# A two-layer recurrent decoder step on one Trainium2 core: the RWKV scans placed link by link between dense products

## The chip, the cores and the metric

The kernel runs on one core of one Trainium2 chip. The core has five engines, each with an instruction stream of its own that it works through in order: TensorE (PE in the profile: matmuls, and PEld for the weight loads beside them), VectorE (DVE), ScalarE (ACT), GpSimd (POOL) and SyncE (SP), which here issues DMAs. They wait for one another by semaphores. The metric is the device time of one execution in microseconds, the median of three runs.

## The reference, cut to what matters

One step of a decoder trunk of two layers for 1024 prompt tokens of a new sequence and 8 sampled tokens, in float32, model width 1024. Layer 0 mixes by Mamba-2 and mLSTM, layer 1 by RWKV-7; each is followed by a SwiGLU of width 2816. The change touches the RWKV-7 scan of the prompt tokens (16 heads of 64):

```python
def _rwkv7_mixer(xn, shift, wkv, p, j):
    x_prev = jnp.concatenate([shift[:, None].astype(xn.dtype), xn[:, :-1]], axis=1)
    xr, xw, xk, xv, xa, xg = (xn + (x_prev - xn) * mu[c] for c in range(6))
    r, k, v = xr @ p['rw_wr'][j], xk @ p['rw_wk'][j], xv @ p['rw_wv'][j]
    ...                                  # decay w, rate a, gate g: low-rank products of xw, xa, xg
    kk = k * p['rw_k_k'][j]; kk = kk / jnp.maximum(jnp.sqrt(jnp.sum(kk * kk, -1, keepdims=True)), 1e-12)
    k = k * (1 + (a - 1) * p['rw_k_a'][j])
    # per head and token, S is 64 x 64 (value x key):
    #   sa = S @ -kk;  S = S * w + sa (kk * a)^T + v k^T;  y = S @ r
    y, new_s = _rwkv7_scan(r, decay, k, v, kk, a, wkv)
    y = (y - mean) * lax.rsqrt(var + RWKV_LN_EPS) * p['rw_ln_w'][j] + p['rw_ln_b'][j]
    y = (y + bonus) * g                  # bonus = sum(r * k * r_k) * v, per head
    return y @ p['rw_wo'][j], (xn[:, -1], new_s)

def _swiglu(x, w_gu, w_down):
    gate, up = jnp.split(x @ w_gu, 2, axis=-1)
    return (jax.nn.silu(gate) * up) @ w_down
```

## The kernel before, in words

**Tokens and stages.** The tokens are worked in two halves, 0 (tokens 0 to 511) and 1 (512 to 1031, the sampled ones among them). In program order: layer 0's mixer for both halves, `ffn(0,0)` (layer 0, half 0), the RWKV projections of half 0 (`rwkv_proj(0)`), `ffn(0,1)`, `rwkv_proj(1)`, `rwkv_out(0)` (output projection of half 0), `ffn(1,0)`, in whose course `rwkv_out(1)` is written at its 21st row block, then `ffn(1,1)` and the final norms.

**Dense products.** Every weight tile of 128 x 128 and every activation is split into a high and a low fp32r part, and a product is three matmuls (`mm3`, L186: low·high, high·low, high·high). `dense_tile` (L189) writes, for one output tile of 128 rows and each block of columns (2 x 260 or 2 x 256 for a half), one chain of eight such terms, 24 matmuls, into a PSUM bank, and then the operations that empty it. The splitting of weights is done by ACT (high, L175) and DVE (low, L145). In an `ffn`, names are `ps_g`, `ps_u` (gate, up), `ps_d` (down, fed by `al`, `ah`, the split of silu(gate)·up), `xb`/`xc` (the residual that `ps_d` is added to), and `f01l`, `f10l` and so on (the normed input).

**The scan of a half** has 16 heads as 8 pairs j (two heads fill 128 partitions), and 8 chunks of 64 tokens. For a pair:

- `rw_pre` (L1231): loads k, w, a, r; DVE and ACT work of 128 x 512 each (names `thw`, `tha`, `cs`, `kk`, `BK`, `al`), one sum over the head on PE (`kks`, its operand split by POOL into `sqh`, `sql`), 8 matmuls `AB` (L1279), whose lower blocks are sent to HBM.
- `rw_inv` (L1309): a 30-step triangular inverse on POOL (`t` and `X`, L145), its result sent to HBM (`scr_tblk`) and loaded again as `obd`, transposed by DVE (L1335), and two sets of matmuls `off` (L1338, L1345) for the corner blocks (`scr_toff`).
- `rw_front` for each group g of 2 chunks: block-diagonal operands (`abd`, `bbd`, `kbd`, `vbd`, `tbd`, one buffer each; `Bb` on POOL), then a chain in which PE and DVE alternate: `av` transposes, products `sc`, masked by DVE into `RD` (L145), product `Z`, copied by DVE (L1396), products `M`, masked by DVE into `rM`.
- `rw_fin` (L1405) for each chunk, the recurrence itself: `fin` (L1421, L1423) in the one PSUM bank of its pool, two ACT copies to `sbd` (L1427), a transpose (L1431), a DVE copy to `ST` (L1433), which the next chunk's L1423 reads, and a DVE copy of the output to `y` (L1436). One `y` buffer serves all pairs.
- `rw_ln`: two sums over the head on PE (`yc`, `yv`, operands split by POOL), the norm, bonus and gate, all on 128 x 512 of `y` in place, which is then stored (`scr_yg`). `rw_bonus` makes `bon`.

**What sets the order.** The tile framework takes the order in which the program is written as priority and fixes from it, at build time, one static order per engine; on the chip an engine doesn't pass an instruction that waits. So where a scan step is written among the dense products decides what it stands behind. Before, the generator `rwkv_scan(hf)` (L1564) yields after whole steps: one start step (`rw_pre`, inverse and bonus of pair 0), then 8 x 4 steps, one per pair and group. A step writes `rw_front` of its group, `rw_fin` for both chunks of the group before it, at g = 1 the next pair's `rw_pre` and the start of its inverse, which is written in pieces (`INV_CUT`), and at g = 2 `rw_ln` of the pair before and the next bonus. Scan 0 goes forward by one step at each of the 22 row blocks f of `ffn(0,1)`, then at places of `rwkv_proj(1)` (`phook`, L1680: c is the projection, j its output tile), with all that is left at c = 3, j = 0. Scan 1 takes 4 steps at odd j of c = 3, and then 9 steps per 5 row blocks of `ffn(1,0)` (`hook`, L1702).

Of the kernel before, what the change touches and what calls it, by code (L numbers as in the profile page):

```python
# [90 lines left out]
def _body(tc, nc, I, O, top):  # L91
# [68 lines left out]
    def sum2(ps, c, src, hi, lo, e=None):  # L160

        split(src, hi, lo, e)
        PE.matmul(out=ps, lhsT=c, rhs=hi, start=True, stop=False)
        PE.matmul(out=ps, lhsT=c, rhs=lo, start=False, stop=True)

# [1014 lines left out]
    INV_CUT = (6, 12, 18)  # L1180
# [11 lines left out]
    def rw_open():  # L1192
# [38 lines left out]
    def rw_pre(hf, j):  # L1231
        base = HALF[hf][0]
        tm, pr, Pt = R_.tm, R_.pr, R_.Pt
        d = Ctx()
# [61 lines left out]
        return d

    def rw_bonus(hf, j, d):
# [9 lines left out]

    def rw_inv(hf, j):  # L1309
# [7 lines left out]
        for c_ in range(1, 31):  # L1317
# [31 lines left out]
    def rw_front(hf, j, d, g):  # L1349
        base = HALF[hf][0]  # L1350
        gpl = R_.gp
        nm = f"{hf}{j}"
# [3 lines left out]
        def gt(s_, n=2, **kw):
            return gpl.tile([128, n, 128], F32, name=f"{s_}{nm}{g}", tag=s_, **kw)

        def mm2(b, o, lhs, rhs):
            for q in range(2):  # L1360
                PE.matmul(out=b[:, o + q * 128:o + q * 128 + 128], lhsT=lhs(q), rhs=rhs(q), start=True, stop=True)  # L1361

        def q2(b, n=2, o=0):
            return b[:, o * 128:(o + n) * 128].rearrange("p (q n) -> p q n", q=n)
# [31 lines left out]
        V.tensor_copy(out=fl(Z), in_=b[:, 0:256])  # L1396
# [8 lines left out]
    def rw_fin(hf, j, d, g, fr):  # L1405
# [9 lines left out]
        for q in range(2):  # L1415
            c = 2 * g + q
# [19 lines left out]
            V.tensor_copy(out=y[:, c * 64:c * 64 + 64], in_=b[:, 0:64])  # L1436
# [127 lines left out]
    def rwkv_scan(hf):  # L1564

        D = {0: rw_pre(hf, 0)}
        for _ in rw_inv(hf, 0):
            pass
        rw_bonus(hf, 0, D[0])
        yield  # L1570
        prev = None
        for j in range(8):
            inv = None
            for g in range(4):
                if g == 1 and j < 7:
                    D[j + 1] = rw_pre(hf, j + 1)
                    inv = rw_inv(hf, j + 1)
                fr = rw_front(hf, j, D[j], g)
                if g == 2 and j:
                    rw_ln(hf, j - 1, D[j - 1])  # L1580
                if g == 2 and j < 7:
                    rw_bonus(hf, j + 1, D[j + 1])
                if prev:
                    rw_fin(hf, *prev)
                prev = (j, D[j], g, fr)
# [94 lines left out]
    def phook(c, j):  # L1680
# [133 lines left out]
```

## Time and profile before

| | us |
|---|---|
| median of three runs | 3510.93 |
| fastest, slowest run | 3500.98, 3512.57 |
| the profiled execution: own time | 3510.93 |
| its span (first to last instruction) | 3509.2 |
| PE busy in the span | 3245.9 |
| DVE busy | 2333.7 |
| POOL busy | 1241.3 |

The execution that was profiled is the median run itself; 1.7 us of it lie outside its span. From the trace, the stages that hold scan work lie at these times from the span's start: `ffn(0,1)` from 1516 to about 2040, then to 2110 its end, the norm and the first product of `rwkv_proj(1)`; `rwkv_proj(1)` to 2357, `rwkv_out(0)` to 2425, `ffn(1,0)` from 2425, with the scan until about 2960. From 3110 `ffn(1,1)` runs without any scan.

How to read the rows: a row of a group has line, engine, operation, out<-in, shape and count, then busy time and mean time of one in ns, then the idle time of the engine just before these instructions and what released it. A row of the timeline has the start, the duration, the instruction, and in brackets the idle time before it. A row of the waits has the instruction that waited, what it waited for, the total, the number of times, and the longest.

### The profile page before, as it was taken

What the parts mean: (1) busy time and instruction counts of PE and PEld (TensorE: products, weight loads), DVE (VectorE), ACT (ScalarE), POOL (GpSimd) and SP (SyncE); (2) the same over time, 40 slices, a digit from 0 to 9 for tenths busy, and PEclk for the clock granted to TensorE, in tenths of its full rate; (3) what the DMA queues carried; (4) which work ended last, traced back from release to release, by engine and by line L of the source; (5) the groups of instructions that cost most, each with busy time, mean ns of one, the idle gap of its engine ahead of it and who ended that gap; (6) DMA issues with size and microseconds to landing.
All of it is one profiled execution on the core that took longest, in us unless ns stands there. A gap on an engine that the chain in (4) does not pass through costs nothing.

```text
span 3509.2 us, 61245 instructions
## 1 busy us (share of the span) xinstructions
PE 3245.9 (92%) x22615; PEld 3000.7 (86%) x22615; DVE 2333.7 (67%) x4315; ACT 1653.4 (47%) x3701; POOL 1241.3 (35%) x1586
## 2 busy tenths in 40 slices
PE   6998899998999999989999968988989999999998
PEld 6987789877778887779999968987888889999998
DVE  8865744466765477676776686667777776575555
ACT  5444435434243245654454555665555644453223
POOL 3257520121200002254644566237677783000000
PEclk9999999999999999999999989998999999999999
DMA  3467665663663343553333324462433333333232
GB/s 117 123 183 217 212 194 150 185 196 128 224 198 109 96 144 108 183 153 98 102 102 94 99 77 131 133 204 73 116 100 98 100 95 109 125 97 97 85 102 67
DMA packets 399135, 458.26 MB, mean 131 GB/s; under 512 B 154756, under 2 KB 295524, under 8 KB 398708
## 3 DMA queue, kind: packets, MB, share of 16 engines
q1 hardware_dynamic: 398836, 454.34, 43.6%
q8 instruction: 179, 2.93, 0.3%
q14 instruction: 120, 0.98, 0.1%
HBM read 352.10 MB, written 102.07 MB: 129 GB/s over the span
## 4 chain that ended last, share of the span: by engine, by line
PE 48%; DVE 11%; POOL 10%; DMA 7%; ACT 5%; issue 4%; SPq 1%; DVEq 0%; ACTq 0%; POOLq 0%
PE ps_g L186 10%; PE ps_u L186 9%; PE ps_d L186 8%; PE ps_rw L186 6%; POOL X L145 4%; POOL t L145 4%; PE ps_out L186 3%; PE ps_o L186 2%; ACT L154 2%; PE ps_wo L186 1%; PE M L1361 1%; DMA phm<-scr_hmt 1%; PE cu L731 1%; PE sc L1361 1%; DMA obd<-scr_tblk 1%
## 5 line engine op out<-in xcount | busy, mean ns | idle before, releaser
L186 PE MATMUL ps_d<-al,dhi 128*128 128x260 f32 (+2 forms) x1248 | 386.5, 310 | 20.4 <-DVE xa L145 6.3
L186 PE MATMUL ps_d<-ah,dhi 128*128 128x260 f32 (+2 forms) x1248 | 373.9, 300 | 0.0
L186 PE MATMUL ps_d<-ah,dlo 128*128 128x260 f32 (+2 forms) x1248 | 373.6, 299 | 0.0
L145 POOL TENSOR_TENSOR X<-X,t 32x30 f32<-32x30 f32 (+14 forms) x480 | 308.6, 643 | 32.7
L145 POOL TENSOR_TENSOR t<-X 32x30 f32<-32x30 f32 (+14 forms) x480 | 297.6, 620 | 30.5
L186 PEld LDWEIGHTS ps_d<-al,dhi 128*128 128x128 f32 x1248 | 237.9, 191 | 40.5 <-DVE xa L145 10.7
L186 PEld LDWEIGHTS ps_d<-ah,dlo 128*128 128x128 f32 x1248 | 238.3, 191 | 7.3
L186 PEld LDWEIGHTS ps_d<-ah,dhi 128*128 128x128 f32 x1248 | 237.9, 191 | 7.3 <-issue 0.2
L145 DVE TENSOR_TENSOR wlo_g<-raw_g,whi_g 128x512 fp32r<-128x512 f32 (+1 forms) x192 | 143.2, 749 | 112.9 <-ACT whi_g L175 105.7
L948 ACT CAST dhi<-rawd 128x1024 fp32r<-128x1024 f32 x88 | 88.4, 1046 | 211.5 <-PE ps_d L186 204.9
L175 ACT CAST whi_g<-raw_g 128x512 fp32r<-128x512 f32 (+1 forms) x192 | 114.0, 599 | 147.7 <-DMA raw_g<-in_wgu 90.6
L154 ACT ACT_TABLE_LOAD x136 | 174.5, 1283 | 6.4 <-DVE ss L145 4.1
L145 DVE TENSOR_TENSOR wlo_u<-raw_u,whi_u 128x512 fp32r<-128x512 f32 x176 | 134.6, 766 | 58.1 <-ACT whi_u L175 57.2
L175 ACT CAST whi_u<-raw_u 128x512 fp32r<-128x512 f32 x176 | 108.0, 619 | 122.7 <-PE ps_u L186 97.4
L186 PE MATMUL ps_in<-xnl,whi_in 128*128 128x344 f32 x480 | 156.4, 326 | 1.0 <-ACT ext L287 1.0
L186 PE MATMUL ps_in<-xnh,whi_in 128*128 128x344 f32 x480 | 155.7, 324 | 0.0
L186 PE MATMUL ps_in<-xnh,wlo_in 128*128 128x344 f32 x480 | 155.3, 324 | 0.0
L145 DVE TENSOR_TENSOR dlo<-rawd,dhi 128x512 fp32r<-128x512 f32 x176 | 128.2, 782 | 15.6 <-ACT dhi L948 15.6
L145 POOL TENSOR_TENSOR xx<-xa 128x512 f32<-128x512 f32 x8 | 9.7, 1244 | 350.7 <-PE ps_out L186 350.7
L157 ACT CAST ah<-sg 128x260 fp32r<-128x260 f32 (+2 forms) x155 | 67.5, 436 | 139.4 <-DVE sg L148 137.6
L145 POOL TENSOR_TENSOR Bb<-Bc,consts 128x256 f32<-128x256 f32 x64 | 53.7, 839 | 219.5 <-PE M L1361 147.0
L145 DVE TENSOR_TENSOR wlo_rw<-raw_rw,whi_rw 128x512 fp32r<-128x512 f32 x96 | 74.2, 778 | 78.2 <-ACT whi_rw L175 77.3
(959 smaller groups left out, 11950.0 us busy)
## 6 DMA issues: line engine op xcount, KB each, us to landing
raw_g<-in_wgu SPq DMA_DIRECT2D x88, 512.0 KB
raw_u<-in_wgu SPq DMA_DIRECT2D x88, 512.0 KB
rawd<-in_wdn SPq DMA_DIRECT2D x88, 512.0 KB
raw_rw<-in_wrw SPq DMA_DIRECT2D x48, 512.0 KB
raw_o<-in_wout SPq DMA_DIRECT2D x32, 512.0 KB
raw_in<-in_win SPq DMA_DIRECT2D x20, 512.0 KB
D<-scr_acr SPq DMA_DIRECT2D x16, 512.0 KB
Cs<-in_mc SPq DMA_DIRECT2D x16, 512.0 KB
```

The costliest lines, as they stand in the source:

```text
L145: (e or V).tensor_tensor(out=out, in0=a, in1=b, op=op)
L154: S.activation(out, a, f, **kw)
L157: S.copy(hi, src)
L175: S.copy(hi[0:p, 0:m], raw[0:p, c0:c0 + m])
L186: PE.matmul(out=ps, lhsT=w[a], rhs=x[b], start=i == 0, stop=i == n - 1)
L731: PE.matmul(out=o, lhsT=ktok[:, (2 * h + k) * 128:(2 * h + k) * 128 + 128], rhs=vw[:, h, :], start=True, stop=True)
L948: S.copy(hi, raw)
L1361: PE.matmul(out=b[:, o + q * 128:o + q * 128 + 128], lhsT=lhs(q), rhs=rhs(q), start=True, stop=True)
```

## The change

The same operations on the same data are written in another order; scan and dense matmuls keep their number and shapes. Five things are new.

**1. A turn per so many columns.** `dense_tile` ends each block of columns with `beside(cols)`, which adds up columns and gives the scan a turn whenever the sum reaches a unit: 8 x 260, one chain of 24 products, for scan 0; 8 x 232 for scan 1. Scan 0 begins before `ffn(0,1)`, scan 1 at c = 3, j = 0 of `rwkv_proj(1)`, where `finish_run` writes what is left of scan 0. The calls of `advance` for the scans are gone.

**2. Three lanes.** A turn moves each of three generators by one link: `fins()` (the recurrence), `fronts()`, and `prepare()` (`rw_pre`, `rw_inv`, `rw_ln` and `rw_bonus`). The functions have new yields, one at each place where PE would need an answer of another engine: before `kks`, `AB`, the second `off`, `Z`, `M`, the transpose of `rw_fin`, each chunk, `yc`, `yv`, `bon`. For this `sum2` is parted into `split` and `add2`. Counted from the program as it is written, a scan takes about 159 turns; of scan 0's, 125 are given before the last row block of `ffn(0,1)`, and it ends before c = 3. By PE's order the chunks of `rw_fin` were spread 44, 20, 0 and 64 over `ffn(0,1)`, `rwkv_proj(1)`, `rwkv_out(0)` and `ffn(1,0)`, and are now 56, 8, 4 and 60.

**3. Operands one group ahead.** `rw_operands`, cut from `rw_front`, loads the next group's operands right behind the copy of `Z`.

**4. The inverse** is written on POOL in one piece (`INV_POOL`), and what follows it 11 turns later (`INV_TURNS`).

**5. Buffers.** `abp` has two; `rw_ln` writes to a tile of its own, `yn`, so that `y` is free when it is split and no longer waits for the store; the copy to `y` stands ahead of the transpose.

```diff
+    def beside(cols):
+        if B_.run is None or B_.busy:
+            return
+        B_.acc += cols
+        while B_.acc >= B_.unit:
+            B_.acc -= B_.unit
+            ...
+            if next(B_.run, 0) == 0:
+                B_.run = None
...
     def dense_tile(w, xs, name, evac, m=128, blocks=NBLK, base=0, th=TA_):
...
             evac(n0, n, o)
+            beside(len(w) * n)
...
-    INV_CUT = (6, 12, 18)
+    INV_POOL, INV_TURNS = 1, 11
...
     def rw_inv(hf, j):
...
-            if c_ in INV_CUT:
-                yield
+        yield
         dma(out=TBLK[hf, j], in_=X)
...
         Z = gt("Z")
         b = bank("Z")
         mm2(b, 0, lambda q: tbd[:, q, :], lambda q: R[:, q, :])
         V.tensor_copy(out=fl(Z), in_=b[:, 0:256])
+        ahead_()
+        yield
         b = bank("M")
...
                 S.copy(sb[hs, hs], b[hs, 64:128])
                 if last:
                     dma(out=O["wkv_p"][hs, j, :], in_=sb[hs, hs])
+            V.tensor_copy(out=y[:, c * 64:c * 64 + 64], in_=b[:, 0:64])
             if not last:
+                yield
                 PE.transpose(b[:, 128:256], sb, ident)
                 d.ST = gpl.tile([128, 128], F32, name=f"ST{nm}{c}", tag="ST")
                 V.tensor_copy(out=d.ST, in_=b[:, 128:256])
...
-            V.tensor_copy(out=y[:, c * 64:c * 64 + 64], in_=b[:, 0:64])
...
         b = pbank("yc")
-        sum2(b, centr, y, *hl[0], G)
+        add2(b, centr, *hl[0])
+        y = tm.tile([128, HT], F32, name="yn" + nm, tag="t6")
         act(y, b, AF.Square)
+        split(y, *hl[1], G)
+        yield
         b2 = pbank("yv")
...
+        def prepare():
+            for j in range(8):
+                yield from till(lambda: s_.front >= 4 * j - 4)
+                yield from rw_pre(hf, j, D[j])
+                inv = rw_inv(hf, j)
+                for _ in range(INV_POOL):
+                    next(inv)
+                t0 = s_.turn
+                if j > 1:
+                    yield from till(lambda: s_.fin >= 4 * j - 4)
+                    yield from rw_ln(hf, j - 2, D[j - 2])
+                yield from rw_bonus(hf, j, D[j])
+                yield from till(lambda: s_.turn >= t0 + INV_TURNS)
+                for _ in inv:
+                    yield
+                s_.ready = j + 1
+                yield
...
+        lanes = [fins(), fronts(), prepare()]
+        while lanes:
+            lanes = [x for x in lanes if next(x, 0) != 0]
+            s_.turn += 1
+            yield 1
...
-    ffn(0, 1, xb, lambda f: advance(steps, 1), pbank, lambda: advance(steps, 1))
+    ffn(0, 1, xb, None, pbank, lambda: begin(rwkv_scan(0), 8 * 260))
...
         if c == 3 and j == 0:
-            advance(steps, 99)
+            finish_run()
+            begin(rwkv_scan(1), 8 * 232)
...
     def hook(f):
-        advance(steps, 9 * (f + 1) // 5 - 9 * f // 5)
```

Three places show what this does to the engines' orders. The first is DVE's order at the end of `ffn(0,1)`, where the last down products are added to the residual (`xb`, L148) ahead of the norm. Before:

```order
L148 SCALAR_TENSOR_TENSOR xb_9318<-xb_9318,cols,n_acc 128x260
L1436 COPY y_20790<-fin_20791 128x64
L151 TENSOR_SCALAR thw_22184<-tha_22186 128x512
L145 TENSOR_TENSOR al_22213<-kk_22205,Pt 128x512
L148 SCALAR_TENSOR_TENSOR xb_9319<-xb_9319,cols,n_acc 128x260
L145 TENSOR_TENSOR n_acc<-n_acc,n_sq 128x260
L145 TENSOR_TENSOR thw_22184<-thw_22184,kk_22205 128x512
L151 TENSOR_SCALAR tha_22186<-tha_22186,hka 128x512
L145 TENSOR_TENSOR RD_21342<-sc,consts 128x512
L145 TENSOR_TENSOR BK_22215<-thw_22184,cs_22201 128x8x64
L145 TENSOR_TENSOR tha_22186<-tha_22186,k_22182 128x512
L1433 COPY ST_20805<-fin_20799 128x128
```

and after:

```order
L148 SCALAR_TENSOR_TENSOR xb_9318<-xb_9318,cols,n_acc 128x260
L1477 COPY y_21123<-fin_21963 128x64
L148 SCALAR_TENSOR_TENSOR xb_9319<-xb_9319,cols,n_acc 128x260
L148 SCALAR_TENSOR_TENSOR xb_9312<-xb_9312,cols,n_acc 128x260
L148 SCALAR_TENSOR_TENSOR xb_9313<-xb_9313,cols,n_acc 128x260
L148 SCALAR_TENSOR_TENSOR xb_9314<-xb_9314,cols,n_acc 128x260
L148 SCALAR_TENSOR_TENSOR xb_9315<-xb_9315,cols,n_acc 128x260
L148 SCALAR_TENSOR_TENSOR xb_9316<-xb_9316,cols,n_acc 128x260
L148 SCALAR_TENSOR_TENSOR xb_9317<-xb_9317,cols,n_acc 128x260
L148 SCALAR_TENSOR_TENSOR xb_9318<-xb_9318,cols,n_acc 128x260
L148 SCALAR_TENSOR_TENSOR xb_9319<-xb_9319,cols,n_acc 128x260
L1482 COPY ST_22007<-fin_21963 128x128
```

The 128 x 512 operations of `rw_pre` and the mask `RD`, which stood between the updates of the norm, have moved away from there; two small copies of `rw_fin` are left.

The second is DVE's order in `ffn(1,0)` at the end of a pair, where `rw_ln` works on the output (`y`, or now `yn`) and PE waits for the copy of `Z` to form `M`. Before:

```order
L145 TENSOR_TENSOR y_27292<-yc,y_27292 128x512
L145 TENSOR_TENSOR RD_28387<-sc,consts 128x512
L151 TENSOR_SCALAR y_27292<-y_27292,cols 128x512
L148 SCALAR_TENSOR_TENSOR sg_7_28734<-sg_7_28734,ps_u_7_0_28789 128x256
L145 TENSOR_TENSOR al_7_28733<-sg_7_28734,ah_7_28732 128x256
L145 TENSOR_TENSOR y_27292<-y_27292,gr_28482 128x512
L145 TENSOR_TENSOR bon_28509<-v_28506,bon 128x512
L151 TENSOR_SCALAR thw_29213<-thw_29213 128x512
L145 TENSOR_TENSOR wlo_u_80_29091<-raw_u_8_29088,whi_u_80_29090 128x512
L1396 COPY Z_28389<-Z 128x256
L1433 COPY ST_28411<-fin_28405 128x128
L1254 SCALAR_TENSOR_TENSOR cs_29230<-rmask,thw_29213 128x512
```

and after:

```order
L145 TENSOR_TENSOR yn_28485<-yc,yn_28485 128x512
L145 TENSOR_TENSOR dh_28955<-dwk_28532,dh_28954 128x256
L145 TENSOR_TENSOR RD_28656<-sc,consts 128x512
L151 TENSOR_SCALAR yn_28485<-yn_28485,cols 128x512
L145 TENSOR_TENSOR xc_2_24842<-xc_2_24842,ps_d_2_0_28617 128x256
L145 TENSOR_TENSOR xc_2_24842<-xc_2_24842,ps_d_2_256_28625 128x256
L145 TENSOR_TENSOR xc_3_24843<-xc_3_24843,ps_d_3_0_28633 128x256
L1477 COPY y_28459<-fin_28690 128x64
L1439 COPY Z_28696<-Z 128x256
L145 TENSOR_TENSOR yn_28485<-yn_28485,gr_28423 128x512
L145 TENSOR_TENSOR xc_3_24843<-xc_3_24843,ps_d_3_256_28658 128x256
L145 TENSOR_TENSOR xc_4_24844<-xc_4_24844,ps_d_4_0_28666 128x256
```

Between the mask `RD` and the copy of `Z` stood seven operations of other work, four of them 128 x 512 of `rw_ln`, `rw_bonus` and `rw_pre`; now there are five, of which one is of that kind.

The third is PE's order in `rwkv_out(0)` at the first `off` of scan 1. With a row's number left out, before:

```order
L186 MATMUL ps_wo07_256_25638<-yg0l0_25129,whi_wo070_25604 128x256
L186 MATMUL ps_wo07_256_25638<-yg0h0_25128,wlo_wo070_25605 128x256
L186 MATMUL ps_wo07_256_25638<-yg0h0_25128,whi_wo070_25604 128x256
L1338 MATMUL off_24342<-obd_13757,oa10_24335 32x128 x4
L186 MATMUL ps_wo07_256_25638<-yg0l1_25131,whi_wo070_25604 128x256
```

and after:

```order
L189 MATMUL ps_wo03_0_25348<-yg0h1_24850,whi_wo030_25340 128x256
L189 MATMUL ps_wo03_0_25348<-yg0l2_24853,whi_wo030_25340 128x256
L189 MATMUL ps_wo03_0_25348<-yg0h2_24852,wlo_wo030_25341 128x256
L1373 MATMUL off_24809<-obd_13759,oa10_24775 32x128 x4
L189 MATMUL ps_wo03_0_25348<-yg0h2_24852,whi_wo030_25340 128x256
```

The `off` matmuls stand behind the output tiles 0 to 2 of the projection now, before behind 0 to 6; counted back to the last `AB` of that pair, 357 dense products lie between, where there were 410.

More of the change, by code (lines that the diff above doesn't have):

```diff
@@ L158, in split, with add2 @@
         tt(lo, src, hi, ALU.subtract, e)
+    def add2(ps, c, hi, lo):
+        PE.matmul(out=ps, lhsT=c, rhs=hi, start=True, stop=False)
+        PE.matmul(out=ps, lhsT=c, rhs=lo, start=False, stop=True)
     def sum2(ps, c, src, hi, lo, e=None):
         split(src, hi, lo, e)
-        PE.matmul(out=ps, lhsT=c, rhs=hi, start=True, stop=False)
-        PE.matmul(out=ps, lhsT=c, rhs=lo, start=False, stop=True)
+        add2(ps, c, hi, lo)
     def wload(src, name, n=1024, step=128, e=None, th=TA_, p=128):
@@ L187, in mm3, with begin, finish_run @@
                 i += 1
+    B_ = Ctx()
+    B_.run, B_.acc, B_.busy = None, 0, False
+    def beside(cols):
[4 more added lines that the diff above has]
+            B_.acc -= B_.unit
+            B_.busy = True
+            if next(B_.run, 0) == 0:
+                B_.run = None
+            B_.busy = False
+            if B_.run is None:
+                break
+    def begin(run, unit):
+        assert B_.run is None
+        B_.run, B_.acc, B_.unit = run, 0, unit
+        next(run)
+    def finish_run():
+        while B_.run is not None:
+            if next(B_.run, 0) == 0:
+                B_.run = None
     def dense_tile(w, xs, name, evac, m=128, blocks=NBLK, base=0, th=TA_):
@@ L1207, in rw_open @@
         for nm in ("abp", "abd", "bbd", "kbd", "vbd", "tbd"):
-            R_.bd[nm] = [fx.tile([128, 2, 128], F32, name=f"{nm}{i}") for i in range(1)]
+            R_.bd[nm] = [fx.tile([128, 2, 128], F32, name=f"{nm}{i}") for i in range(2 if nm == "abp" else 1)]
             for t in R_.bd[nm]:
@@ L1256, in rw_pre @@
         act(cs, cs, AF.Exp, scale=C2)
+        yield
+        b = pbank("kks")
+        add2(b, onesr, sqh, sql)
+        ts(sq, b, 1e-24, ALU.max)
+        act(sq, sq, AF.Ln)
+        act(sq, sq, AF.Exp, scale=-0.5)
         kk = tmp(6, "kk")
@@ L1347, in rw_inv, with rw_operands @@
         dma(out=TOFF[hf, j].rearrange("(g u) i l -> (u i) g l", u=4), in_=A)
-    def rw_front(hf, j, d, g):
+    def rw_operands(hf, j, d, g):
         base = HALF[hf][0]
-        gpl = R_.gp
-        nm = f"{hf}{j}"
-        abd, bbd, kbd, vbd, tbd = (R_.bd[n_][g % len(R_.bd[n_])] for n_ in ("abd", "bbd", "kbd", "vbd", "tbd"))
+        abd, bbd, kbd, vbd, tbd = (R_.bd[n_][0] for n_ in ("abd", "bbd", "kbd", "vbd", "tbd"))
         gs_ = slice(2 * g, 2 * g + 2)
[L1356 to L1364, printed above, removed]
         half_bd(abd, d.al[:, gs_])
@@ L1564, in rwkv_scan @@
     def rwkv_scan(hf):
[L1566 to L1585, printed above, removed]
-                if inv:
-                    advance(inv, 1 if g < 3 else 9)
-                yield
@@ L1589, in rwkv_scan, with till @@
-        rw_fin(hf, *prev)
-        rw_ln(hf, 7, D[7])
+        s_ = Ctx()
+        s_.turn = s_.front = s_.fin = s_.ready = 0
+        D = {j: Ctx() for j in range(8)}
+        ops, res = {}, {}
+        def till(f):
+            while not f():
+                yield
+        def prepare():
[12 more added lines that the diff above has]
+                for _ in inv:
+                    yield
+                s_.ready = j + 1
+                yield
+            for j in (6, 7):
+                yield from till(lambda: s_.fin >= 4 * j + 4)
+                yield from rw_ln(hf, j, D[j])
@@ new lines, in operands, with fronts @@
+        def operands(i):
+            if i < 32 and i not in ops and s_.ready > i // 4:
+                ops[i] = rw_operands(hf, i // 4, D[i // 4], i % 4)
+        def fronts():
+            for i in range(32):
+                yield from till(lambda: s_.ready > i // 4 and s_.fin >= i - 1)
+                if i not in ops:
+                    operands(i)
+                    yield
+                res[i] = yield from rw_front(hf, i // 4, D[i // 4], i % 4, ops.pop(i), lambda: operands(i + 1))
+                s_.front = i + 1
+                yield
@@ L1592, in advance, with fins @@
+        def fins():
+            for i in range(32):
+                yield from till(lambda: s_.front > i)
+                yield from rw_fin(hf, i // 4, D[i // 4], i % 4, res.pop(i))
+                s_.fin = i + 1
+                yield
+        lanes = [fins(), fronts(), prepare()]
[3 more added lines that the diff above has]
+            yield 1
     def advance(steps, n):
@@ L1702, in hook @@
     def hook(f):
[L1703 removed]
         dec_hook(f)
         if f == 20:
[L1707 removed]
+            finish_run()
             rst.close()
```

58 lines of the change are left out of this document (34 added, 24 removed).

## The prediction
> **What bounds the kernel now.** I read the page's busy shares first, then the windows of the stages with scan work beside one without, then PE's waits there, then the timeline around the longest.
>
> ```profile
> PE 3245.9 (92%) x22615; PEld 3000.7 (86%) x22615; DVE 2333.7 (67%) x4315; ACT 1653.4 (47%) x3701; POOL 1241.3 (35%) x1586
> ```
>
> PE is busy for 92% of the span, and the change keeps its matmuls. Only PE's idle time, and time at a lower clock, can go.
>
> ```profile
> 1516.00:2040.00 524.00, 499.23 (x4098) 485.87 (x4097) 368.59 (x755) 268.02 (x631) 295.01 (x443) 0.99 0.37 103
> 2054.90:2089.00 34.10, 11.55 (x44) 9.70 (x45) 32.35 (x51) 14.12 (x32) 26.55 (x41) 0.50 0.19 50
> 2425.00:2960.00 535.00, 489.06 (x3988) 466.24 (x3989) 405.63 (x793) 293.14 (x729) 372.57 (x548) 0.95 0.35 94
> 3110.00:3509.00 399.00, 383.07 (x3182) 381.56 (x3180) 234.80 (x506) 128.36 (x239) 0.00 (x0) 0.98 0.30 93
> ```
>
> Columns: window, length, busy time of PE, PEld, DVE, ACT, POOL, granted clock, DMA. PE is idle 25 us in `ffn(0,1)` (first row), 46 in `ffn(1,0)` (third), 16 without a scan (fourth). In the second row, around the norm, 34.1 us hold 11.55 of PE work at half clock. The clock columns cost more: 1% of 524 is 5 us, 5% of 535 is 27. PE's waits in `ffn(1,0)`:
>
> ```profile
> PE M L1361 <- DVE Z L1396: 8.4, 9, 3.1
> PE fin L1421 <- DVE y L1436: 7.6, 5, 2.9
> ...
> PE fin L1421 <- DVE RD L145: 3.7, 1, 3.7
> ...
> PE off L1345 <- DMA obd<-scr_tblk: 0.3, 1, 0.3
> ```
>
> The rows of scan matmuls, twelve from first to last, sum to 34.6 us; in `ffn(0,1)` seven sum to 13.8:
>
> ```profile
> PE yv L164 <- POOL y L145: 5.9, 5, 2.2
> ...
> PE Z L1361 <- DMA tbd<-scr_toff: 0.3, 1, 0.3
> ```
>
> A pair of heads costs (13.8 + 5) / 5.5 = 3.4 us in `ffn(0,1)` and (34.6 + 27) / 8 = 7.7 in `ffn(1,0)`. So the recurrence isn't the limit; what bounds the scan stages is dense PE work plus short waits for DVE and the clock behind them.
>
> **The change part by part.** All terms are against the profiled execution, 3510.93 us, which is the median run.
>
> **A, the norm ahead of `rwkv_proj(1)`.**
>
> ```profile
> L148 DVE SCALAR_TENSOR_TENSOR xb<-xb,cols,n_acc 128x260 f32<-128x260 f32 x16 | 15.2, 1008 | 0.5 <-ACT n_acc L154 0.5
> L1254 DVE TENSOR_TENSOR_SCAN cs<-rmask,thw 128x512 f32<-128x512 f32 x1 | 1.6, 1595 | 0.0
> ...
> L1396 DVE COPY Z<-Z 128x256 f32<-128x256 f32 x1 | 0.4, 410 | 0.0
> 2066.04 0.80 PE L1421 MATMUL fin<-RD,av 128*128 128x128 f32 x2 [12.66 <-DVE y L1436]
> ...
> 2083.01 0.58 PE L1279 MATMUL AB<-BK,abp 128*128 128x128 f32 x1 [9.14 <-DVE BK L145]
> ```
>
> The first three rows are DVE's groups from 2057.1 to 2083.3, where it idles 1.5 us. Thirteen of them, from `cs` to `Z`, are scan work that stood between the updates of `xb`: 10.1 us, and 1.0 idle ahead of one. PE had nothing else (12.66 and 9.14 idle). In DVE's order after the change about 1.2 us of scan copies is left: −10. But 44 PE records ran in that hole for nothing; most must now stand beside dense work, at most 44 x 0.12 = 5, I take 4. **−6**; ends −10 and 0.
>
> **B, DVE's bursts and the `y` store in `ffn(1,0)`.** The longest wait of `M`, with what DVE did before:
>
> ```profile
> 2663.45 1.23 PE L1361 MATMUL M<-Z,av 128*128 128x128 f32 x4 [3.08 <-DVE Z L1396]
> 2660.03 1.08 DVE L145 TENSOR_TENSOR y<-y,gr 128x512 f32<-128x512 f32 x1
> 2661.04 0.68 DVE L145 TENSOR_TENSOR bon<-v,bon 128x512 f32<-128x512 f32 x1
> ...
> 2662.98 0.41 DVE L1396 COPY Z<-Z 128x256 f32<-128x256 f32 x1
> 2950.40 0.23 DVE L1436 COPY y<-fin 128x64 f32<-128x64 f32 x1 [3.05 <-DMA scr_yg<-y]
> ```
>
> A whole step wrote the end of a pair, the next bonus and the start of `rw_pre` together, so the `Z` copy stood behind all of it, and in the last row the first `y` copy of a pair stood behind the store of the one buffer. The links part the bursts; `yn` frees `y`. The three rows of waits for `Z`, `y` and `RD` are 8.4 + 7.6 + 3.7 = 19.7 us. Behind three of these waits the clock fell:
>
> ```profile
> 2587.40:2590.80 3.40, 3.40 (x18) 3.40 (x17) 1.87 (x4) 2.95 (x9) 3.01 (x6) 0.50 0.95 320
> 2662.50:2672.70 10.20, 9.25 (x52) 9.02 (x52) 9.89 (x17) 6.25 (x11) 7.31 (x11) 0.50 0.41 108
> 2816.10:2822.90 6.80, 6.76 (x40) 6.45 (x40) 6.80 (x13) 6.62 (x17) 4.96 (x7) 0.50 0.24 67
> ```
>
> That is 20.4 us at half clock, so 10.2 lost. Together 30. DVE remains loaded (405.63 of 535), and a link that waits now stops only its own lane in the writing, yet all of PE on the chip; so I take half: **−15**, ends −30 and 0. What is late next are the waits for dense operands, which stay.
>
> A wait need not fill a clock stretch of 3.4 us to be followed by one:
>
> ```profile
> 1530.53 0.39 PE L186 MATMUL ps_g<-f01l,whi_g 128*128 128x260 f32 x1 [1.75 <-ACT whi_g L175]
> 1532.70:1536.10 3.40, 3.02 (x14) 2.72 (x14) 3.40 (x6) 2.77 (x5) 3.09 (x5) 0.50 0.00 0
> ```
>
> Here a stretch at half clock follows a wait of 1.75 us, 2 us later. The Trainium skill, "TensorE: Matmul & The Clock Gate", "Part 1: The HAM clock gate", says that the clock halves only after a whole idle window of about 3.4 us; by that the short waits would leave the clock alone and B would be half of 19.7, about −10. This trace disagrees, and the sum goes by the trace.
>
> **C, chunks moved.** By PE's order 12 chunks more of the recurrence (1.5 pairs) run in `ffn(0,1)`, 4 fewer in `ffn(1,0)`, 8 fewer in the projections. At one price per pair this is **0**; at 3.4 and 7.7 it is 1.5 x 3.4 − 0.5 x 7.7 − 3.4 = −2.
>
> **D, the first inverse of scan 1.**
>
> ```profile
> 2409.86 0.66 PE L1338 MATMUL off<-obd,oa 128*32 128x128 f32 x8 [5.40 <-DVE obd L1335]
> 3012.66 0.28 PE L186 MATMUL ps_u<-f10l,whi_u 128*128 128x256 f32 x1
> 3012.78 0.28 PE L186 MATMUL ps_u<-f10h,wlo_u 128*128 128x256 f32 x1
> ```
>
> `off` waited 5.40 us already; dense matmuls follow at 0.12. Between that pair's last `AB` and `off` stand 357 of them instead of 410: 53 x 0.12 = **+6**; ends 0 (an earlier inverse) and +10, with the clock.
>
> **E, `yv`.** The next link is at least one turn away, 24 x 0.12 = 2.9 us, above the longest of its waits (2.2). Half of 5.9 goes: **−3**; ends −6 and 0.
>
> **F, the tail.**
>
> ```profile
> 3013.01 0.33 PE L1554 MATMUL yvd<-d_kk,onesr 128*128 128x64 f32 x2
> 3027.31 0.39 PE L186 MATMUL ps_wo<-mix10l,whi_wo 128*128 128x260 f32 x1 [1.22 <-DVE mix10l L145]
> ```
>
> From the sampled tokens' `yvd` to the first product of `rwkv_out(1)` 14.3 us pass; 89 dense matmuls cover it now instead of 108: 19 x 0.12 = **+2.5**; ends 0 and +2.5.
>
> The operands a group ahead, the second `abp` and the inverse in one piece cost POOL and DMA the same instructions. POOL is busy 372.57 of 535 us; without that cover an inverse late by some us would show at `off`, where D is. I put them at 0.
>
> Sum: −6 − 15 + 0 + 6 − 3 + 2.5 = −15.5, so **3495 us**.
>
> **The rivals.**
>
> *Better.* All of B goes (−30), with half of the scan's other 14.9 us of waits there (−7), A is −10, E −6, and D and F cost nothing: −53, 3458. For it: each of these waits is under one turn and a half. Against it: DVE's total is unchanged. Between 3458 and 3485, centre 3472.
>
> *The waits only move; the change doesn't part what it says.* PE's order has 2,548 runs of scan matmuls between dense ones, before 2,550; in `ffn(1,0)` the dense work between `fin` and its transpose grows from 2.7 to 3.2 us at the median, but from `Z` to `M` it shrinks from 2.9 to 2.5. The scheduler had interleaved the steps already. Then B is 0: −6 + 6 − 3 + 2.5, 3510.
>
> *The clock doesn't follow the waits.* If half clock comes from another cause than these waits, B is −10 and the sum −10.5: 3500. The row at 1532.70 speaks against it. This is the skill's rule of that section, in time.
>
> *Slower: DVE's queue in `ffn(0,1)` thickens.* It has 56 chunks now, 7 pairs, as dense as `ffn(1,0)`. DVE's share, 70% there, goes towards `ffn(1,0)`'s 76%; beside more POOL work each operation of DVE is longer:
>
> ```profile
> L145 DVE TENSOR_TENSOR al<-sg,ah 128x260 fp32r<-128x260 f32 x44 | 25.3, 575 | 7.2 <-ACT ah L157 7.2
> L145 DVE TENSOR_TENSOR al<-sg,ah 128x256 fp32r<-128x256 f32 x34 | 25.4, 748 | 4.8 <-ACT ah L157 4.8
> ```
>
> The same operation takes 575 ns with POOL busy for 56% of the stage, 748 with 70%. (The Trainium skill, "SBUF — State Buffer", "Who interferes with whom", calls the port pair that DVE and POOL share an exclusive lock; the rows agree in direction.) Then a pair costs 7.7 there too: 7 x 7.7 − 19 = +35, less 0.5 x 7.7 and 3.4 for what left the other stages; with A, D and F, and without B and E: +30, 3541. It decides when DVE's answer to `Z` or `fin` takes longer than the 2.5 us of dense work up to the next link.
>
> **How the numbers follow.** Chances: forecast 0.30, better 0.20, moved waits 0.24, clock apart 0.07, slower 0.19. A measurement of this kernel tells about 0.3%, 10.5 us, from no change: faster is below 3500.4, slower above 3521.5. Faster: 0.20 of the forecast (its own range is 3485 to 3508), 0.20, 0.05 of the moved waits, 0.03: 0.48. Slower: 0.19 and 0.02 of the moved waits: 0.21. Same: 0.31. The range goes from the better case's end, 3458, to 3535, under the slower rival's centre; that leaves out some 0.05 below and 0.13 above.
>
> **What would show it.** A: no hole of 9 us in PE ahead of `rwkv_proj(1)`. B: the waits for `Z`, `y` and `RD` in `ffn(1,0)` at some 10 us, its clock above 0.96, no wait on the `y` store. D: the first `off` waits 10 us or more. E: `yv` below 3 us. F: `rwkv_out(1)` waits 3 to 4 us. The forecast is wrong if `ffn(0,1)` shows more than 30 us of scan waits, or a clock under 0.97, or if new waits of `Z` or `off` for a DMA appear.

## The result and the profile after

The changed kernel is slower: 3544.99 us median of four runs (3537.18 to 3549.57) against 3510.17 (3500.98 to 3512.57), a ratio of 1.0106 with a 95% interval of 1.0088 to 1.0124. (The ratios, here and below, are those on record with their intervals. They are not the quotients of the medians beside them, here 1.0099, and differ from these by up to 0.12%.) The forecast was 3495 us, its range 3458 to 3535. The profiled execution took 3540.84 us with a span of 3539.1; the stages below are of it.

The busy shares of the page after:

```profile
PE 3263.0 (92%) x22615; PEld 3013.9 (85%) x22615; DVE 2326.2 (66%) x4315; ACT 1659.4 (47%) x3705; POOL 1225.1 (35%) x1587
```

The same 22,615 matmuls keep PE busy 17 us longer (3245.9 before). The granted clock over the span, 0.967 before and 0.965 after, accounts for some 8 us of that (an estimate: 3.3% of 3509 is 116 us, 3.5% of 3539 is 124); where the rest comes from was not found. The windows of the four stages with scan work, before, from the first gate product of `ffn(0,1)` to that of `ffn(1,1)`; the columns are window, length, busy time of PE, PEld, DVE, ACT, POOL, clock, DMA:

```profile
1516.50:2088.20 571.70, 518.88 (x4194) 501.96 (x4193) 411.33 (x824) 291.86 (x680) 333.14 (x496) 0.96 0.36 101
2088.20:2356.80 268.60, 238.89 (x1859) 229.48 (x1859) 178.94 (x352) 172.32 (x440) 110.48 (x145) 0.95 0.50 149
2356.80:2425.20 68.40, 56.34 (x439) 53.84 (x437) 48.10 (x78) 32.78 (x75) 55.09 (x83) 0.87 0.40 110
2425.20:3110.70 685.50, 636.42 (x5214) 610.45 (x5214) 498.60 (x1003) 362.26 (x868) 377.70 (x553) 0.96 0.35 99
```

and after, with the same boundaries in the program:

```profile
1514.80:2120.60 605.80, 547.06 (x4406) 525.87 (x4404) 447.90 (x889) 329.03 (x777) 380.87 (x576) 0.97 0.37 102
2120.60:2380.90 260.30, 224.90 (x1662) 213.55 (x1662) 172.25 (x309) 155.22 (x380) 82.16 (x101) 0.93 0.48 147
2380.90:2458.60 77.70, 66.20 (x520) 63.84 (x520) 47.18 (x88) 38.40 (x90) 59.02 (x97) 0.92 0.35 97
2458.60:3140.30 681.70, 628.58 (x5123) 604.35 (x5123) 473.13 (x986) 353.50 (x841) 342.33 (x508) 0.95 0.35 99
```

The rows are `ffn(0,1)` with the norm behind it, `rwkv_proj(1)`, `rwkv_out(0)`, and `ffn(1,0)` with `rwkv_out(1)`. `ffn(0,1)` holds 212 PE records more and is 34.1 us longer. `rwkv_proj(1)` holds 197 fewer and is only 8.3 us shorter, at a lower clock. `rwkv_out(0)` is 9.3 us longer with 81 more. `ffn(1,0)` is 3.8 us shorter with 91 fewer. The sum is +31.3 us. So the first place to look is where the scan's matmuls stand.

The first window holds two opposite changes. Parted behind the last up product of `ffn(0,1)`, it is, before (two rows) and after:

```profile
1516.50:2030.50 514.00, 489.69 (x4022) 476.76 (x4022) 359.55 (x739) 262.90 (x618) 286.30 (x430) 0.99 0.37 104
2030.50:2088.20 57.70, 29.19 (x174) 25.20 (x172) 51.78 (x86) 28.96 (x63) 46.85 (x67) 0.71 0.25 75
1514.80:2082.50 567.70, 526.05 (x4251) 506.86 (x4250) 413.11 (x820) 309.88 (x732) 345.51 (x521) 0.98 0.37 105
2082.50:2120.60 38.10, 21.00 (x157) 19.01 (x156) 34.80 (x70) 19.15 (x45) 35.36 (x56) 0.80 0.23 70
```

`ffn(0,1)` alone is 53.7 us longer, with 36.4 us more of PE work and 17.3 us more of idle PE; the stretch around the norm is 19.6 us shorter. In `ffn(0,1)` the waits of scan matmuls rose from 13.3 to 30.8 us. The three largest rows after are these; the two of `fin` have no counterpart in this stage before:

```profile
PE fin L1480 <- DVE y L1477: 9.6, 9, 3.4
PE AB L1318 <- DVE BK L145: 4.9, 3, 3.3
PE fin L1468 <- DVE ST L1482: 4.8, 5, 2.8
```

PE's waits in `rwkv_proj(1)` say why it gave back so little. Before:

```profile
PE ps_rw L186 <- DVE xc1l L145: 4.9, 4, 2.3
PE l2ps L1060 <- ACT l2t L154: 3.7, 1, 3.7
PE l2ps L1060 <- ACT rst L1084: 2.9, 2, 2.3
PE ps_rw L186 <- ACT rst L1084: 2.6, 3, 2.2
```

and after:

```profile
PE ps_rw L189 <- ACT rst L1115: 9.2, 3, 5.4
PE ps_rw L189 <- DVE xc1l L145: 8.7, 8, 1.9
```

The projection waits for its own operands: `xc1l`, the split of the mixed input, and `rst`, the copies that empty its PSUM banks. These two rows grew from 7.5 to 17.9 us with fewer of the scan's matmuls between; all waits of the dense products there grew from 24 to 32 us.

In `ffn(1,0)`, the waits for `Z`, `y` and `RD` that the prediction summed to 19.7 us, and those that came:

```profile
PE M L1419 <- DVE Z L1439: 7.0, 4, 2.4
PE sav L162 <- ACT dh L157: 5.4, 4, 2.8
PE fin L1468 <- DVE ST L1482: 4.7, 4, 2.2
PE bon L162 <- ACT rh L157: 4.3, 2, 2.3
...
PE fin L1480 <- DVE y L1477: 0.9, 1, 0.9
...
PE fin L1468 <- DVE RD L145: 0.4, 1, 0.4
```

`y` fell from 7.6 to 0.9 and `RD` from 3.7 to 0.4, but `ST` and `rh` are new and `sav`, of the sampled tokens, rose; the clock is 0.95 where it was 0.96. The row of `rh` has a plain origin. In ACT's and PE's timelines, and in the window behind them (last row):

```profile
2591.84 0.62 ACT L157 CAST rh<-r 128x512 fp32r<-128x512 f32 x1 [2.91 <-DMA scr_yg<-yn]
2592.51 0.51 PE L162 MATMUL bon<-rh,onesr 128*128 128x512 f32 x1 [2.05 <-ACT rh L157]
2593.60:2600.20 6.60, 5.89 (x33) 5.14 (x34) 5.94 (x11) 3.46 (x9) 5.59 (x7) 0.50 0.24 67
```

The new tile `yn` has the tag `t6`, and so has `rh` of the next `rw_bonus` (and `sqh` of the next `rw_pre`). The wait for the store was taken from `y`, where it held DVE for 4.2 us in all, and given to `rh`, where it stops ACT's whole queue:

```profile
DVE y L1436 <- DMA scr_yg<-y: 4.2, 3, 3.1
ACT rh L157 <- DMA scr_yg<-yn: 15.0, 5, 3.3
```

(first row before, second after, both of the whole execution). Of these 15.0 us PE shows 4.3, in `bon`; behind the wait of 2.05 us PE ran 6.6 us at half clock.

### The profile page after: what moved, and what is told of

The parts are those of the page before. It is cut to its first block, busy times and chain, and to the rows that moved or that the text cites. A ratio compares the mean times of both kernels' runs of the same rounds, so it can differ in the third digit from the quotient of the medians.

```text
span 3539.1 us, 61233 instructions
## 1 busy us (share of the span) xinstructions
PE 3263.0 (92%) x22615; PEld 3013.9 (85%) x22615; DVE 2326.2 (66%) x4315; ACT 1659.4 (47%) x3705; POOL 1225.1 (35%) x1587
## 4 chain that ended last, share of the span: by engine, by line
PE 56%; DVE 15%; DMA 11%; ACT 7%; POOL 6%; issue 4%; SPq 2%; DVEq 0%; ACTq 0%; POOLq 0%
PE ps_g L189 11%; PE ps_d L189 10%; PE ps_u L189 9%; PE ps_rw L189 5%; PE ps_in L189 4%; PE ps_out L189 2%; ACT L154 2%; PE ps_wo L189 2%; POOL t L145 2%; POOL X L145 2%; PE ps_o L189 2%; DVE lp L148 1%; PE ps_z L189 1%; PE M L1419 1%; DMA phm<-scr_hmt 1%
## 5 line engine op out<-in xcount | busy, mean ns | idle before, releaser
L189 PE MATMUL ps_d<-al,dhi 128*128 128x260 f32 (+2 forms) x1248 | 392.4, 314 | 15.7 <-DVE xa L145 6.1
L145 POOL TENSOR_TENSOR t<-X 32x30 f32<-32x30 f32 (+14 forms) x480 | 288.2, 600 | 30.4
L145 DVE TENSOR_TENSOR wlo_u<-raw_u,whi_u 128x512 fp32r<-128x512 f32 x176 | 142.6, 812 | 61.0 <-ACT whi_u L178 59.1
L189 PE MATMUL ps_rw<-xc1l,whi_rw 128*128 128x260 f32 x384 | 114.3, 302 | 21.1 <-ACT rst L1115 9.2
```

The lines of the kernel that those rows point to most:

```text
L145: (e or V).tensor_tensor(out=out, in0=a, in1=b, op=op)
L189: PE.matmul(out=ps, lhsT=w[a], rhs=x[b], start=i == 0, stop=i == n - 1)
```

## The experiments

Each ratio is to the kernel before on the same chip, with its 95% interval. Scan matmuls by stage are counted in PE's order as the framework fixed it from the program; the expectations call this the written order.

**Unit 8 x 330.** `begin(rwkv_scan(0), 8 * 330)` instead of `8 * 260`.

> The changed kernel with one number changed: the unit of scan 0 is 8 x 330 columns instead of 8 x 260, so that the written order gives ffn(0,1) about 598 scan matmuls and rwkv_proj(1) 228 (changed kernel 728 and 114, kernel before 603 and 229). Theory P (the time follows the stage in which the scan's matmuls stand; in rwkv_proj(1) they fill holes that are there anyway, in ffn(0,1) they lengthen it): the holes of rwkv_proj(1) close again, about 13 us of its waits and clock and most of the 28 us in ffn(0,1) against 20 us of work come back, 3515 to 3530. Rival L (the writing by links costs by itself, wherever it stands): 3538 to 3548, as the changed kernel.

3529.77 us against 3513.9, 1.0033 (1.0017 to 1.0049). With the shares of the stages as before the change, two thirds of the loss are gone; theory P, at its slow end. `rwkv_out(0)` took 72.7 us, 68.4 before.

**Early placement in the kernel before.**

```diff
-    ffn(0, 1, xb, lambda f: advance(steps, 1), pbank, lambda: advance(steps, 1))
+    ffn(0, 1, xb, lambda f: advance(steps, 2 if f % 4 == 1 else 1), pbank, lambda: advance(steps, 1))
```

> The kernel before, with whole steps, but scan 0 takes two steps instead of one at every fourth row block of ffn(0,1): the written order then has 726 scan matmuls in ffn(0,1) and 112 in rwkv_proj(1), as in the changed kernel (728 and 114). Theory P: slower than before by 15 to 30 us, 3525 to 3541. Rival L: within 6 us of before, 3505 to 3517.

3531.32 us, 1.0044 (1.0027 to 1.0060). The kernel with whole steps loses too when its scan stands where the change puts it. Its first two windows, between the same boundaries:

```profile
1528.50:2121.70 593.20, 546.32 (x4407) 526.17 (x4405) 437.34 (x876) 317.18 (x758) 371.99 (x569) 0.97 0.37 101
2121.70:2378.80 257.10, 222.13 (x1657) 212.48 (x1658) 170.49 (x308) 153.77 (x379) 82.57 (x97) 0.94 0.47 148
```

213 records more make `ffn(0,1)` with the norm 21.5 us longer, 202 fewer make `rwkv_proj(1)` 11.5 us shorter: the same pattern without one line of the new code. Here too the first window holds two changes, `ffn(0,1)` 43.9 us longer and the stretch around the norm 22.4 shorter. But in `ffn(0,1)` the scan's waits did not rise (12 us), and in `rwkv_proj(1)` the two rows above sum to 8.3 us only: the times of the stages repeat, the waits behind them don't. `rwkv_out(0)`, with 54 records more, is 8.6 us longer, `ffn(1,0)`, with 65 fewer, 2.5 shorter. The four stages together are 16 us longer.

**The copy to `y` behind the transpose.** The line `V.tensor_copy(out=y[...], in_=b[:, 0:64])` moved back to the end of the chunk.

> The changed kernel with the copy to y behind the transpose and the ST copy again, as in the kernel before. Theory Y (the copy ahead of the transpose makes PE wait twice per chunk for DVE: 14.1 us of waits of the transpose L1480 for y in ffn(0,1), none of that kind before): the waits of the transpose for DVE go, 10 to 20 us faster than the changed kernel, 3525 to 3535. Rival: the wait moves to the next fin, which needs the one PSUM bank back: 3538 to 3548, as the changed kernel.

3549.55 us, 1.0092 (1.0071 to 1.0113), not to be told from the changed kernel. The changed kernel's wait in `ffn(0,1)` and the norm:

```profile
PE fin L1480 <- DVE y L1477: 14.1, 10, 4.5
```

and in this run:

```profile
PE fin L1468 <- DVE y L1484: 13.7, 9, 3.3
```

The rival was right in its time, and in part in its reason: the waits of the recurrence for DVE, 27.5 us in the changed kernel (14.1, and 13.4 of `fin` for `ST`), became 13.7 and 4.0 of the transpose for ACT's `sbd`, and the rest came back at other instructions, `yc` and the dense products among them. PE's idle time in the stretch is 57.5 us, 58.7 in the changed kernel.

**`rh` in another tile.**

```diff
-        rh, rl = tmp(6, "rh", F32R), tmp(2, "rl", F32R)
+        rh, rl = tmp("rv", "rh", F32R), tmp(2, "rl", F32R)
```

> The changed kernel with rh of rw_bonus in the tile tag of sql instead of that of yn, so that it no longer waits for the store of yn. Theory R (the wait for the y store was not removed but handed to rh, on ACT's queue: bon waited 4.3 us for rh in ffn(1,0), with half-clock stretches of 6.8 and 3.4 us behind): 4 to 10 us faster than the changed kernel, 3535 to 3541. Rival: off the path, within 3 us of 3545.

3535.7 us, 1.0052 (1.0033 to 1.0070). The median is in theory R's range, but by the ratios the gain is 0.54%, some 19 us, for 4.3 us of waits and the clock behind them. Nor did ACT's stop go: `sqh` of the next `rw_pre` has the tag `t6` too, and waited instead, without any wait of PE for it:

```profile
ACT sqh L157 <- DMA scr_yg<-yn: 11.2, 7, 3.1
```

**`yn` instead in that tile** (`tag="rv"` for `yn`).

> The changed kernel with yn, instead of rh, moved to the tile tag of sql: rh no longer waits for the store of yn, and the written order stays nearly that of the changed kernel (728, 114, 71 and 735 scan matmuls in the four stages; 728, 114, 75 and 731 there). Theory R (rh's wait holds ACT's queue): the same gain as moving rh, a ratio to before of 1.003 to 1.007. Rival (moving rh gained by another order, 57 instead of 75 in rwkv_out(0) and 743 instead of 731 in ffn(1,0), not by the wait): 1.009 to 1.012.

3537.66 us, 1.0070 (1.0051 to 1.0090). Parting the two tiles gains in either way, here somewhat less; 1.0070 is the end of what theory R gave, and the rival's 1.009 stands at the end of the interval.

**Unit 8 x 330 with `rh` moved.**

> Unit 8 x 330 for scan 0 and rh in the tile tag of sql, together. If theories P and R are separate mechanisms, the gains add: 0.7% and 0.5% less than the changed kernel's 1.0106, a ratio to the kernel before of 0.995 to 1.001. If R's gain hung on the crowded ffn(0,1) of the changed kernel, nothing is added to the 1.0033 of the unit alone: 1.001 to 1.005.

3555.83 us, 1.0115 (1.0094 to 1.0136): a miss by both. PE's waits in `rwkv_out(0)`:

```profile
PE n_ps L243 <- DVE n_acc L145: 13.5, 2, 12.3
PE kks L162 <- ACT sqh L157: 11.0, 1, 11.0
```

`rwkv_out(0)` took 90.5 us instead of 68.4. At this unit 21 turns are left when c = 3 begins, and `finish_run` writes them in one heap ahead of scan 1; the end of scan 0 and the first `rw_pre` of scan 1 then stand in `rwkv_out(0)` and in the norm behind it. The heap alone is not the cause: with the unit alone the same 21 turns are left, and `rwkv_out(0)` took 72.7 us. Of the two rows, that of `n_ps` was there at 10.7 us; that of `kks` was not.

**Unit 8 x 380 with `rh` moved.**

> As the one before with a unit of 8 x 380: by the written order 515 scan matmuls in ffn(0,1) and 301 in rwkv_proj(1), where there were 600 and 222. Theory P, with rwkv_proj(1) giving back only part of the scan's work in time as long as it has holes (0.56 us for each 1 us of work in the run with two steps at every fourth block): about 15 us of PE work moves, 5 to 8 us faster than with 8 x 330. Rival: the holes of rwkv_proj(1) are filled, and what stands there then waits on its own norm and splits: no gain, or slower by up to 8 us.

3562.33 us, 1.0139 (1.0121 to 1.0157), with 39 turns left for the heap: theory P doesn't go on in this direction, and the rival holds.

**The kernel before, later** (`advance(steps, 0 if f % 6 == 5 else 1)` in `ffn(0,1)`).

> The kernel before, whole steps, but scan 0 pauses at every sixth row block of ffn(0,1): 544 scan matmuls there and 270 in rwkv_proj(1) by the written order (603 and 229 before). Theory P: some 10 us of PE work move to where it costs about half, 2 to 6 us faster than before. Rival (rwkv_proj(1) has no holes left): the same or slower by up to 5 us.

3544.27 us, 1.0096 (1.0075 to 1.0117): worse than both expectations. In its trace `ffn(0,1)` with the norm is 19.5 us shorter, but `rwkv_proj(1)` 11.5, `rwkv_out(0)` 24.8 and `ffn(1,0)` 9.4 us longer.

**No heap: 8 x 330, then 8 x 170.** `B_.unit = 8 * 170` is set at c = 5 of `rwkv_proj(1)`.

> Unit 8 x 330 in ffn(0,1), 8 x 170 from rwkv_proj(1) on, rh in the tile tag of sql. With 8 x 330 throughout, 21 turns of scan 0 were left at c = 3 and written in one heap there (0 in the changed kernel); now 0 are left, and ffn(0,1) keeps its 600 scan matmuls. Theory F (the heap ahead of scan 1's begin is what cost: kks waited 11.0 us and the norm 12.3 us in rwkv_out(0)): the 22 us that rwkv_out(0) had grown go, a ratio to before of 0.998 to 1.004. Rival (a scan that ends late in rwkv_proj(1) costs, heap or not): 1.008 to 1.014.

3534.61 us, 1.0074 (1.0053 to 1.0095). `rwkv_out(0)` fell to 73.1 us as theory F says, but `rwkv_proj(1)` rose from 268.6 (before) to 303.0: between both expectations.

**8 x 300, then 8 x 210.**

> As the one before with 8 x 300 and 8 x 210: 670 scan matmuls in ffn(0,1), 172 in rwkv_proj(1), 0 turns left. Theory P with F: between the run with rh alone (1.0052) and the one with 8 x 330 and 8 x 170: 1.000 to 1.005. Rival (ffn(0,1)'s share of the scan doesn't matter once nothing is left in a heap): both of these and the run with rh alone alike within 0.2%.

3544.26 us, 1.0093 (1.0072 to 1.0114): not between its neighbours, and outside both expectations.

**The kernel before, later, without the heap** (as above, and `advance(steps, 2 if c == 2 else 1)`).

> The kernel before with scan 0 pausing at every sixth row block of ffn(0,1), as in the earlier run, but two steps instead of one at the four places of c = 2 in rwkv_proj(1), so that scan 0 has taken all of its steps before c = 3 instead of three being left there. Theory F: the heap was the loss of 0.96%; without it 0.998 to 1.003. Rival (rwkv_proj(1) holds no more scan work without loss): 1.006 to 1.012.

3533.24 us, 1.0069 (1.0047 to 1.0090). The rival holds. `rwkv_out(0)` fell from 93.1 to 72.0 us, so the heap explains a part; `rwkv_proj(1)` grew to 301.4 us here too.

**Scan 0 in whole steps, scan 1 by links.** The functions of the kernel before serve scan 0 at their old places.

> Scan 0 in whole steps at the places of the kernel before, scan 1 by links as in the changed kernel with rh in the tile tag of sql (613, 225, 55 and 755 scan matmuls in the four stages by the written order). Theory S (the loss is made where scan 0 stands, in ffn(0,1) and rwkv_proj(1), while links in ffn(1,0) gain once rh is free: rwkv_out(0) and ffn(1,0) together took 746 to 754 us in the runs with links and a free rh, 754 before): 0.995 to 1.000 of the kernel before. Rival (the links lose in scan 1 too): 1.003 to 1.009.

3541.03 us, 1.0073 (1.0057 to 1.0089). Theory S falls: `rwkv_out(0)` and `ffn(1,0)` took 762.0 us, 8.1 more than before, and `ffn(0,1)` with the norm, whose scan is written as before, 583.0 instead of 571.7. In PE's order it is not quite as before (613 scan matmuls, 603 before), and in `ffn(0,1)` alone the scan's waits are 22 us, 13.3 before; what moved the order was not found.

**Unit 8 x 330 with `yn` moved.**

> The changed kernel with the unit 8 x 330 for scan 0 and yn in the tile tag of sql (602, 223, 23 and 800 scan matmuls by the written order). With the unit alone the ratio was 1.0033; with the unit and rh moved 1.0115, where a heap of 21 turns ran into rwkv_out(0). If theory R holds whatever the unit: 0.998 to 1.002. If the place of the heap decides and R adds nothing to be seen beside it: 1.003 to 1.012.

3518.8 us, 1.0022 (1.0005 to 1.0039), between both expectations and the fastest version by links. With the unit alone it was 1.0033: here parting the tiles gains nothing that the intervals show, though `rh` had waited 15.7 us on ACT there. The same heap of 21 turns is written, and `rwkv_out(0)` took 76.5 us. Against the same kernel with 8 x 260 (1.0070) the placement is worth 0.48%.

**The kernel before with `yn`.**

```diff
+        y = tm.tile([128, HT], F32, name="yn" + nm, tag="t6")
         act(y, b, AF.Square)
```

> The kernel before with one thing of the change: rw_ln writes to yn in the tile tag that rh of the next rw_bonus uses too. Theory R: rh then waits on ACT for the store of yn, and what y no longer waits is given back: 1.001 to 1.006 of before. Rival (term B of the prediction: the first y copy of a pair no longer waits for the store, 7.6 us of waits for y in ffn(1,0)): 0.995 to 0.999.

3527.57 us, 1.0051 (1.0034 to 1.0068). Term B's rival is out: the store of `y` was no cost worth its removal, and PE's wait for `y` in `ffn(1,0)`, 7.6 us before, is still 6.1. Theory R's number is met, and ACT does stop for the store:

```profile
ACT rh L157 <- DMA scr_yg<-yn: 17.7, 8, 4.1
```

But no wait of PE for `rh` is in the trace (of an execution of 3515.52 us, the shortest of six, so that it may lack what costs). The order moved with the tile (619, 213, 36 and 774 scan matmuls; 603 and 229 in the first two before), so the tile isn't all that differs, and the run can't say which of the two costs.

**Both in the kernel before.**

> The kernel before with two steps at every fourth row block of ffn(0,1) and with yn: both suspected costs of the change in the kernel with whole steps (726, 112, 56 and 748 scan matmuls; changed kernel 728, 114, 75 and 731). If early placement (1.0044 alone) and the shared tile together make up the change's 1.0106, and the links themselves add nothing: 1.007 to 1.011. If the links are what costs beyond the placement: 1.003 to 1.006.

3534.21 us, 1.0078 (1.0059 to 1.0096). Early placement and the shared tile, put into the kernel with whole steps, make three quarters of the change's 1.06%. PE waited 1.4 us for `rh` here, ACT 22.4 for the store.

## Why the prediction was wrong, point by point

**Three steps failed: C, which was put at 0; B, which was put at −15; and the price of a pair in `ffn(0,1)`, which the forecast left at 3.4 us and the slower rival alone raised.**

**C, chunks moved.** The prediction priced only a pair's waits, and put its matmuls at nothing wherever they stand. The runs show that the place has a price: with early placement alone the kernel before loses 0.44%, 15 us. From 8 x 260 to 8 x 330 the kernel with links gains 0.48% with `yn` moved and 0.73% with no tile moved, but loses 0.63% with `rh` moved, so the price isn't a matter of these counts alone. The term belonged at about +15. The prediction had the numbers to see it: `rwkv_proj(1)` has 30 us of idle PE in 269, of which its own operands cause 24.

**B, bursts and the `y` store.** Measured: no gain. The waits named fell from 19.7 to 8.3 us (7.0, 0.9 and 0.4), but PE's idle time in the stage rose from 49 to 53 us. Waits of PE passed on to other instructions, as the run with the copy to `y` moved back shows in `ffn(0,1)`, and the store's wait passed to `rh`, which was not looked for: a tile of its own by name was a shared one by tag. The kernels with the shared tag are slower by 0.54% or 0.36% by the two ways of parting the tiles at 8 x 260, by 0.34% in the kernel before with early placement and 0.51% without, and by nothing to be seen at 8 x 330. That ACT's stop is what costs is not shown: it stayed at 11.2 us in the run that gained 0.54%, and with 15.7 us at 8 x 330 there was no loss. With every such tile PE's order moved too.

**Together.** Placement of 0.44% to 0.48% and the tile, with the order that it brings, of 0.34% to 0.54% make 0.8% to 1.0% of the 1.06%. With early placement and no shared tile, links give 1.0052 or 1.0070 and whole steps 1.0044: what the links themselves cost is 0.1% to 0.3%, within the intervals of these runs. By stage, in one execution each, this is the difference of two larger things: `ffn(0,1)` with the norm takes 607.6 or 605.3 us by links and 593.2 by whole steps, `ffn(1,0)` 673.7 or 677.5 and 683.0. The sums are not exact: at 8 x 330 parting the tiles gained 0.11% one way, within the error, and lost 0.82% the other way.

**A, the norm.** Right in direction, and more than was put: from the last up product of `ffn(0,1)` to `rwkv_proj(1)` 38.1 us pass, 57.7 before. PE's records there fell only from 174 to 157, so the matmuls of the +4 hardly left. But whole steps placed early shorten the stretch as much, to 35.3 us: it comes with C's placement. Two holes of scan work stayed, one of them nearly the 9 us that the prediction had excluded:

```profile
2108.19 0.47 PE L1480 MATMUL fin<-consts,sbd 128*128 128x128 f32 x1 [4.49 <-DVE y L1477]
2116.81 0.80 PE L1468 MATMUL fin<-RD,av 128*128 128x128 f32 x2 [8.15 <-DVE ST L1482]
```

The two small copies left in DVE's order take little, but stand behind the updates of `xb`.

**D, the first inverse.** Wrong in sign: `off` waited 3.47 us, where 5.40 had been and 10 were expected.

```profile
2405.39 0.52 PE L1373 MATMUL off<-obd,oa 128*32 128x128 f32 x8 [3.47 <-DVE obd L1370]
```

The 53 matmuls were the wrong measure of the cover. From the end of that pair's last `AB` (2344.4, and 2341.8 after) to the start of the wait 60.1 us pass before and 60.1 after: other work and other waits fill what the dense products left. The chain behind `AB` came back 1.9 us sooner; why was not found.

**E, `yv`.** Right for this row: 5.9 us became 0.7; but other waits of the scan there rose by more. **F, the tail.** Right in direction, about a third in size: `rwkv_out(1)` waited 1.99 us, 0.8 more than before, where 2.5 were put.

**The slower rival** named the place and, with 3541, almost the time, at a chance of 0.19; its reason is half of what happened. In `ffn(0,1)` the scan's waits rose from 13.3 to 30.8 us, past the 30 that the prediction had set as a sign against itself, while the pairs rose from 5.5 to 7: 2.4 us a pair became 4.4, and the new rows are waits of `fin` for DVE. With whole steps at the same early places they are 12 us, so this part comes with the links. The near agreement in time is luck: A, E and the placement came out otherwise than the rival had them. That DVE's operations grow longer beside more POOL work did come true:

```profile
L145 DVE TENSOR_TENSOR al<-sg,ah 128x260 fp32r<-128x260 f32 x43 | 28.4, 660 | 5.5 <-ACT ah L157 5.4
```

660 ns where it was 575, with POOL busy for 61% of the stage instead of 56%. That the waits of `fin` come from it is not shown.

**What stays open.** All sixteen other versions were slower than the kernel before, by 0.22% to 1.39%, the one with a single tile changed by 0.51%, and not in the order of any one count. So a rival is left: that any move away from this order loses a few tenths of a per cent, whatever moved it. The runs don't part this from the price of early placement, which one version with whole steps has by itself and one with the shared tile. As to counts, `rwkv_proj(1)` took 303 us with 408 scan records and 268.4 with 377. Which part of its order decides this was not found.

## What to carry to other kernels

Work that is moved costs what its new stage has no room for, less what its old stage can give back; price it by the idle time of both stages, and by what the old stage waits for once the filler is gone. A new tile that shares a tag passes its wait to the next writer of that tag, on whichever engine that is: read who else uses the tag before costing the wait as gone, and then whether the engine that bounds the time waits for it. When a wait of PE for DVE is removed by moving one copy, look for the next instruction that needs the same bank. And part a window that holds two stages before saying that its waits did not grow.

## What the runs showed of the hardware

The length of the same DVE subtraction (`al` from `sg` and `ah`, 128 x 256 or 260) rises with POOL's share in four stages: 426 ns without POOL (`ffn(1,1)` before), 575 ns at 56%, 660 at 61%, 748 at 70%; the other engines' shares are not the same in these stages. And a stretch of 6.6 us at a granted clock of 0.50 began 1 us after a single wait of 2.05 us, much as behind the 1.75 us in the kernel before. The traces before and after hold 36 and 46 stretches at 0.50, 234 and 251 us in all; ahead of each, the waits of PE that reach into the last 3.4 us sum to 0.9 us or more.
